# Decoder layer: memory rows and the first key weights loaded and used in halves, one key block more ahead of the stream's rows

## The chip, the cores and the metric

The kernel runs on one core of a Trainium2 chip. The metric is the device time of one execution in microseconds (us). The core has a matrix engine (PE; PEld is its weight load), a vector engine (DVE), a scalar engine (ACT), GpSimd (POOL), and a queue engine (SP) that issues nearly all DMAs here. Every engine works through its own list of instructions in order, and semaphores hold an instruction until what it needs is there.

## The reference, cut to what matters

One decoder layer, batch 1, 1024 tokens, model width 1024, 256 memory tokens. The change touches only the normalisation of the memory and of the stream's rows, and the keys and values of the memory:

```
def rms_norm(x, g):
    y = x * rsqrt(mean(x * x, axis=-1) + 1e-6)
    return y * g

h     = rms_norm(x, norm_mix_pre)            # 1024 x 1024, then h @ w_in
mem_n = rms_norm(mem, norm_mem)              # 256 x 1024
kv    = mem_n @ w_mem_kv                     # 1024 -> 512 keys | 512 values
k_m, v_m = split(kv, 2)                      # 4 heads of 128
s = einsum('bshd,bmhd->bhsm', q, k_m) * 128 ** -0.5
o = einsum('bhsm,bmhd->bshd', softmax(s), v_m)
```

The rest of the layer (differential attention, pooling, gates, output projection, convolutional channel mixer) follows and is the same in both kernels.

## The kernel before

**Names.** Everything is float32, with 128 rows to a tile. Memory rows are two tiles, m0 and m1 (128 x 1024 each, 512 KB), the stream's rows eight tiles, x0 to x7. The key and value weights come as eight blocks of 512 KB: w0 to w3 are 128 key columns each (`rawm0` to `rawm3`), w4 to w7 are 256 rows each of the value weights. `gp` (named g in the load order) is the gain of the stream's norm, `gm` the gain of the memory's norm, turned into a column by the matrix engine (`pg`).

**Load order.** All loads of the first stage are issued by SP in the order of a list of names, `ORDER` (line 33):

```
ORDER = "m0 m1 w0 w1 x0 g x1 w2 x2 w3 x3 x4 w4 x5 x6 w5 x7 w6 w7 q0 u0".split()
```

**First stage (lines 375 to 640), before.** PE first turns the identity matrix ten times into an unused bank (`keep(10)`, tile `idle`), then the gain (`pg`). It transposes all of m0 and m1 in 16 instructions (line 429; tiles `pt` and `pt2`), and three more unused ones. DVE and ACT multiply the transposed pieces by the gain into `memt` (line 442 on DVE, two calls per half and row tile; line 439 on ACT, four pieces). ACT squares the raw memory rows and sums them (line 418), takes the root (line 133), and five small DVE instructions make the reciprocal norms. These are not multiplied into `memt`: DVE spreads them into `rcol` (line 463), PE transposes `rcol` into a row (`pr`, line 469), ACT copies it (`rrow`, line 470), and the keys are scaled with that row afterwards (`keys_scaled`, line 541).

`keys(j)` multiplies weight block j with `memt` over eight slices of 128 into one bank `pk` (line 536). The trace counts each of these float32 products as two PE instructions, so a block has 16. The banks come from a pool of two, so block j+2 may start only when block j's bank has been read by `keys_scaled(j)`. Beside it every row tile of the stream is squared on ACT, its norm found (`norms`), scaled on DVE into `xn` (line 505), transposed on PE (`turn_row`, line 511, 8 instructions) and split into a high and a low part (lines 520 and 524). `values(a, b)` is 16 products of 512 columns into two banks `pv` (line 556), 32 PE instructions.

The order on each engine is the order of the calls at lines 573 to 640: a helper `on(engine, fn)` chains each instruction behind the one called before it on the same engine. So the list of calls is the plan; later stages (`query`, `pool_in` and so on) are ordered by the compiler around it.

Of the kernel before, what the change touches and what calls it, by code (L numbers as in the profile page):

```python
# [15 lines left out]
P = 128  # L16
D = 1024
# [12 lines left out]
C_K = 1024  # L30
PAD = 24
KEEP = (10, 0, 3)
ORDER = "m0 m1 w0 w1 x0 g x1 w2 x2 w3 x3 x4 w4 x5 x6 w5 x7 w6 w7 q0 u0".split()
C_V = 2048
C_U = 3072
C_QM = 3584
# [5 lines left out]
def kernel(  # L42
# [40 lines left out]
    def bank2(shape=(P, 2 * H), name="b2"):  # L83
        return ps2.tile(list(shape), F32, tag="b2", name=name)
# [255 lines left out]
    def chunk(w, c0, n=P):  # L340
        return w[:, c0:c0 + n].rearrange("(k p) c -> p k c", p=P)
# [6 lines left out]
    with tc.tile_pool(name="kvm", reuse_waits="tile", bufs=1, side="right") as kvp:  # L348
# [5 lines left out]
        with tc.tile_pool(name="pa", reuse_waits="tile", bufs=2, side="right") as pa, \  # L354
# [27 lines left out]
            for what in ORDER:  # L382
                if what == "g":
                    gp = pa.tile([P, D], F32, name="gp", bufs=1)
                    nc.sync.dma_start(out=gp, in_=norm_mix_pre[0:1, :].partition_broadcast(P))
                elif what in ("q0", "u0"):
                    ahead[what[0]] = wload(chunk(w_in, C_QM if what == "q0" else C_U), [P, KT, P])
                elif what[0] == "w":
# [23 lines left out]
            def on(engine, fn):  # L412

                with tc.issue_after(order[engine].ins):
                    order[engine] = fn()

            def square(src, acc):
                on("act", lambda: nc.scalar.activation(
                    out=bank2(name="junk"), in_=src, func=AF.Square, accum_out=acc))

            turned = {}
            for i in range(2):
                both = bank2((P, KT, P), "pt2") if i else None
                for g4 in range(2):
                    pt = both[:, 4 * g4:4 * g4 + 4] if i else bank((P, 4, P), "pt")
                    for j in range(4):
                        k = 4 * g4 + j
                        with tc.issue_after(roots["pe"].ins):
                            roots["pe"] = nc.tensor.transpose(pt[:, j, :], xts["m%d" % i][:, k * P:(k + 1) * P], ident)
# [15 lines left out]
            st = small.tile([P, 5, 2], F32, tag="sb2", name="sb", bufs=2)  # L445
            for i in range(2):
                square(xts["m%d" % i], st[:, 0, i:i + 1])
            gained(0, 0, False)
            gained(1, 0, False)
            gained(0, 1, True)  # L450
            gained(1, 1, False)
            with tc.issue_after(order["act"].ins), tc.issue_after(order["dve"].ins):
                rm = rstd_rest(st)

            for e, n in (("dve", "rstd"), ("act", "last")):
                order[e] = roots[n]
            order["pe"] = roots["pe"]
# [4 lines left out]
            for i in range(2):  # L462
                on("dve", lambda: nc.vector.tensor_scalar(
                    out=rcol[:, i, :], in0=ident, scalar1=0.0, scalar2=rm[i], op0=ALU.mult, op1=ALU.add))

            def norms_row():
                pr = bank((P, NM), "pr")
# [97 lines left out]
            def weights_split(name):  # L565
# [22 lines left out]
            keys_scaled(1)  # L588
            highs("x0")
            lows("x0")  # L590
            keys_high(1)
            keys_low(1)
            squares(["x3"], 1, 2)
            norms(["x2", "x3"])
            scaled("x2")
            keys(2)
            turn_row("x1")
            keys_scaled(2)
            highs("x1")
            lows("x1")  # L600
            keys_high(2)
            keys_low(2)
            scaled("x3")
            squares(["x4", "x5"])
            keys(3)
            turn_row("x2")
            keys_scaled(3)
            norms(["x4", "x5"])
            highs("x2")
            lows("x2")  # L610
            keys_high(3)
            keys_low(3)
            scaled("x4")
            squares(["x6"], 0, 2)
            values(0, 4)
            turn_row("x3")
            scaled("x5")
            highs("x3")
            lows("x3")
            squares(["x7"], 1, 2)  # L620
            norms(["x6", "x7"])
            scaled("x6")
            values(4, 7)
            turn_row("x4")
            highs("x4")
            lows("x4")
            scaled("x7")
            values(7, 10)
            turn_row("x5")
            highs("x5")  # L630
            lows("x5")
            weights_split("q")
            values(10, 13)
            turn_row("x6")
            highs("x6")
            lows("x6")
            values(13, 16)
            values_split(0)
            turn_row("x7")
            highs("x7")  # L640
            lows("x7")
# [1139 lines left out]
```

## Time and profile before

| what | value |
|---|---|
| median of 3 runs | 1730.08 us (1729.88 to 1730.09) |
| the profiled execution | 1730.37 us |
| its span on the core | 1728.4 us |
| PE busy | 1713.0 us, 99% |
| DVE, ACT, POOL busy | 72%, 51%, 3% |
| PE from its first transpose of the memory to the first stream row turned | 4.25 to 15.35 us of the span |

The span is the time from the core's first to its last instruction; 1.97 us of the profiled execution lie around it. The profile's views used here are the page, the chain of waits (from the last instruction back to what released it), the timeline of one engine, the DMA issues of a stretch with the time from issue to landing, and busy time by stretches.

### The profile page before, as it was taken

Reading aid. Unit: us, or ns where it says so; the run is one execution under the profiler, and the core shown is the slowest. Engines: PE = TensorE matmul, PEld = TensorE weight load, DVE = VectorE, ACT = ScalarE, POOL = GpSimd, SP = SyncE. Lnnn points to the kernel's source line nnn. Section 1 sums busy time; section 2 is a strip of 40 time slices with the busy share of each in tenths; the row PEclk is TensorE's granted clock in tenths of the full one; section 3 lists DMA queues with packets and bytes.
Section 4 is the critical chain, followed back from the end, with each engine's and each line's share of the span. In section 5 each row is a group of like instructions: output and inputs, shape, how many; then the busy total and the mean of one; then the engine's idle time right before and its main releaser. Section 6 shows DMA issues by size and latency. Waiting matters only on the chain.

```text
span 1728.4 us, 22402 instructions
## 1 busy us (share of the span) xinstructions
PE 1713.0 (99%) x8106; PEld 1420.5 (82%) x8106; DVE 1240.8 (72%) x2047; ACT 886.2 (51%) x1577; POOL 45.0 (3%) x103
## 2 busy tenths in 40 slices
PE   9999999999999999999999999999999999999998
PEld 7888888887888888888888878888888888888886
DVE  6765875666666578888866555848888888878466
ACT  6434554344544467777744344645555555543453
POOL 0000000000000011111110000000000000000000
PEclk9999999999999999999999999999999999999999
DMA  8883544444874686665556571562433322583344
GB/s 280 309 292 114 162 146 143 162 146 152 263 223 155 207 229 176 174 181 150 143 200 228 183 219 49 170 225 92 127 111 104 122 90 94 194 302 102 108 148 141
DMA packets 232803, 294.41 MB, mean 170 GB/s; under 512 B 15865, under 2 KB 161526, under 8 KB 230006
## 3 DMA queue, kind: packets, MB, share of 16 engines
q1 hardware_dynamic: 229158, 285.61, 51.8%
q0 software_dynamic: 3520, 7.38, 1.2%
q8 instruction: 64, 1.05, 0.2%
q14 instruction: 45, 0.37, 0.1%
q10 hardware_dynamic: 16, 0.00, 0.0%
HBM read 201.10 MB, written 85.56 MB: 166 GB/s over the span
## 4 chain that ended last, share of the span: by engine, by line
PE 91%; DVE 5%; DMA 2%; ACT 1%; issue 1%; SPq 0%; DVEq 0%; ACTq 0%
PE pa L98 8%; PE pa L99 8%; PE pa L100 8%; PE pb L99 5%; PE pb L98 5%; PE pb L100 5%; PE pss L1145 3%; PE pd L98 2%; PE pd L99 2%; PE pd L100 2%; PE poa L1201 2%; PE pe L99 2%; PE pe L98 2%; PE pe L100 2%; PE pya L100 2%; PE pya L98 2%
## 5 line engine op out<-in xcount | busy, mean ns | idle before, releaser
L89 ACT ACTIVATE wpage<-s 128x512 fp32r<-128x512 f32 x136 | 85.3, 627 | 107.5 <-DVE s L183 44.6
L90 DVE TENSOR_TENSOR wpage<-s,wpage 128x512 fp32r<-128x512 f32 x136 | 92.7, 687 | 43.3 <-ACT wpage L89 43.3
L1549 DVE SCALAR_TENSOR_TENSOR cvt<-gv,cols,cvt 128x1023 f32<-128x1023 f32 x88 | 112.4, 1278 | 15.7 <-ACT cvt L1545 15.7
L1149 DVE CUSTOM_DVE_ANT_0 z<-pss,hbias 128x256 f32<-128x256 f32 (+7 forms) x128 | 94.5, 752 | 25.1 <-PE pss L1145 23.9
L1154 ACT ACTIVATE z<-z,mx 128x256 f32<-128x256 f32 (+7 forms) x128 | 98.8, 773 | 21.2 <-DVE mx L1149 21.0
L98 PE MATMUL pa<-T,wpage 128*128 128x512 f32 x264 | 102.8, 390 | 0.0
L99 PE MATMUL pa<-T,wpage 128*128 128x512 f32 x264 | 102.7, 389 | 0.0
L100 PE MATMUL pa<-T,wpage 128*128 128x512 f32 x264 | 102.7, 389 | 0.0
L1145 PE MATMUL pss<-ks,q 128*128 128x512 f32 (+5 forms) x384 | 86.6, 349 | 1.4 <-DVE mx L1149 1.4
L89 ACT ACTIVATE page<-blk 128x1024 fp32r<-128x1024 f32 (+1 forms) x42 | 41.5, 990 | 85.2 <-PE pe L99 50.6
L90 DVE TENSOR_TENSOR page<-blk,page 128x1024 fp32r<-128x1024 f32 (+1 forms) x42 | 47.5, 1131 | 38.2 <-ACT page L89 38.1
L1145 PEld LDWEIGHTS pss<-ks,q 128*128 128x128 f32 x384 | 62.9, 189 | 11.1 <-DVE mx L1149 6.2
L98 PE MATMUL pd<-page 128*128 128x512 f32 x176 | 68.6, 390 | 0.5 <-ACT row L1662 0.5
L99 PE MATMUL pd<-page 128*128 128x512 f32 x176 | 68.5, 389 | 0.0
L100 PE MATMUL pd<-page 128*128 128x512 f32 x176 | 68.3, 389 | 0.0
L98 PE MATMUL pa<-hT,wpage 128*128 128x512 f32 x168 | 65.5, 390 | 0.8 <-DVE gq L210 0.8
L100 PE MATMUL pa<-hT,wpage 128*128 128x512 f32 x168 | 65.4, 389 | 0.0
L99 PE MATMUL pa<-hT,wpage 128*128 128x512 f32 x168 | 65.4, 389 | 0.0
L1201 PEld LDWEIGHTS poa<-aT,v 128*128 128x128 f32 x480 | 60.7, 190 | 3.2 <-ACT srow L1221 1.4
L1201 PE MATMUL poa<-aT,v 128*128 128x256 f32 (+1 forms) x480 | 62.6, 281 | 0.0
L98 PEld LDWEIGHTS pa<-T,wpage 128*128 128x128 f32 x264 | 49.5, 188 | 10.6 <-DVE gv L243 0.3
L100 PEld LDWEIGHTS pa<-T,wpage 128*128 128x128 f32 x264 | 49.6, 188 | 10.3
(429 smaller groups left out, 4964.1 us busy)
## 6 DMA issues: line engine op xcount, KB each, us to landing
q<-q_d SPq DMA_DIRECT2D x64, 256.0 KB, 5.2
wd<-in_w_down_dram SPq DMA_DIRECT2D x22, 512.0 KB, 4.6
tw_d<-wd SPq DMA_DIRECT2D x11, 1024.0 KB
rawv<-in_w_up_dram SPq DMA_DIRECT2D x22, 512.0 KB, 5.7
rawu<-in_w_up_dram SPq DMA_DIRECT2D x22, 512.0 KB, 3.9
ff_d<-cvt SPq DMA_DIRECT2D x22, 512.0 KB, 5.1
blk<-ff_d SPq DMA_DIRECT2D x20, 512.0 KB, 7.4
br<-tw_d SPq DMA_DIRECT2D x20, 512.0 KB, 4.9
```

The source lines that it names most:

```text
L89: copy = nc.scalar.activation(out=hi, in_=src, func=AF.Copy)
L90: nc.vector.tensor_tensor(out=lo, in0=src, in1=hi.bitcast(F32), op=ALU.subtract)
L98: nc.tensor.matmul(o, ah, bh, start=first, stop=False, skip_group_check=onto)
L99: nc.tensor.matmul(o, ah, bl, start=False, stop=False, skip_group_check=onto)
L100: return nc.tensor.matmul(o, al, bh, start=False, stop=last, skip_group_check=onto)
L1145: last["scores"] = nc.tensor.matmul(pss[:, i * H:i * H + m], q[:, j, c, ts], keys, start=(j == 0), stop=(j == 1))
L1149: nc.vector.tensor_tensor_reduce(out=halves(z[:, 0:n]), in0=pss.rearrange("p (a m) -> p a m", a=2)[:, 0:parts, 0:m], in1=halves(biases[h][ ...
L1154: nc.scalar.activation(out=z[:, 0:n], in_=z[:, 0:n], func=AF.Exp, scale=-1.0, bias=mx[:, c:c + 1], accum_out=sm if c else sums[:, h, t:t + 1])
L1201: nc.tensor.matmul(po[:, qs], (vh, vl)[i][:, k, :], w[j][:, ws], start=(n == 0), stop=(n == len(terms) - 1))
L1549: nc.vector.scalar_tensor_tensor(out=cv[:, sh:], in0=u[:, 0:S - sh], scalar=w, in1=cv[:, sh:], op0=ALU.mult, op1=ALU.add)
```

## The change

Both memory row tiles and w0 are loaded in two transfers each (256 KB: half of the columns of a row tile, four of the eight slices of w0; the transfers of m0 and m1 then bring 2 KB for a row at a time and not 4 KB). The load order becomes m0a, m1a, w0a, m0b, m1b, w0b, w1, x0, w2, g, x1, w3, x2, x3, x4, w4 and on. PE turns the first halves of m0 and m1, does the first four slices of `keys(0)`, turns the second halves, does the first four slices of `keys(1)`, then the norms' row `pr`, then the second halves of `keys(0)` and `keys(1)`. Before, it turned both rows whole, did six slices of `keys(0)`, `pr`, the other two slices, and `keys(1)`. The three unused transposes behind the memory rows go. After that the keys run one block ahead of the rows: `keys(2)` stands before the turn of x0, `keys(3)` before that of x1, and the values begin before that of x2. The squares of m0 and m1 wait for the second halves, and the squares of x0 stand behind the copy `rrow` on ACT.

```
-ORDER = "m0 m1 w0 w1 x0 g x1 w2 x2 w3 x3 x4 w4 x5 x6 w5 x7 w6 w7 q0 u0".split()
+ORDER = "m0a m1a w0a m0b m1b w0b w1 x0 w2 g x1 w3 x2 x3 x4 w4 x5 x6 w5 x7 w6 w7 q0 u0".split()
...
+                elif what[2:]:
+                    e = "ab".index(what[2])
+                    if what[0] == "w":
...
+                        nc.sync.dma_start(
+                            out=raws[0].rearrange("p (k c) -> p k c", c=P)[:, e * H4:(e + 1) * H4, :],
+                            in_=chunk(w_mem_kv, 0)[:, e * H4:(e + 1) * H4, :])
+                    else:
...
+                        nc.sync.dma_start(out=xts[n][:, hs], in_=mem[int(n[1]) * P:(int(n[1]) + 1) * P, hs])
...
-            for i in range(2):
-                both = bank2((P, KT, P), "pt2") if i else None
-                for g4 in range(2):
+            def turn_memory(g4):
+                for i in range(2):
...
-                keep(KEEP[1 + i])
...
+            keys(0, 0, H4)
+            turn_memory(1)
+            memory_norms()
+            keys(1, 0, H4)
+            norms_row()
             squares(["x0"])
+            keys(0, H4)
+            keys(1, H4)
             norms(["x0"])
-            keys(0, 0, 6)
-            norms_row()
-            keys(0, 6)
             keys_scaled(0)
             scaled("x0")
-            squares(["x1"])
             keys_high(0)
             keys_low(0)
+            keys_scaled(1)
+            squares(["x1"])
+            keys_high(1)
+            keys_low(1)
             norms(["x1"])
             scaled("x1")
-            keys(1)
+            keys(2)
             turn_row("x0")
```

`memory_norms` holds the squares, the second `memt` pieces, the root, the reciprocals and `rcol`, unchanged in themselves.

On PE, at the start of the program, this stood before (`pt` and `pt2` are the turned memory rows, `pk` the keys, `pr` the norms' row, `rawm0` and `rawm1` the weight blocks w0 and w1):

```order
L404 MATMUL pg_185<-ident_80,grow_128 128x8
L429 MATMUL pt_189<-ident_80,xt_132 128x128 x4
L429 MATMUL pt_194<-ident_80,xt_132 128x128 x4
L429 MATMUL pt2_199<-ident_80,xt_134 128x128 x8
L399 MATMUL idle_174<-ident_80 128x128 x3
L536 MATMUL pk_241<-memt_127,rawm0_136 128x256 x6
L469 MATMUL pr_248<-ident_80,rcol_229 128x128 x2
L536 MATMUL pk_241<-memt_127,rawm0_136 128x256 x2
L536 MATMUL pk_269<-memt_127,rawm1_138 128x256 x8
L511 MATMUL pt_278<-ident_80,xn_256 128x128 x4
```

The same place on PE in the changed kernel, up to the first turn of a stream row:

```order
L418 MATMUL pg_188<-ident_80,grow_128 128x8
L444 MATMUL pt_193<-ident_80,xt_132 128x128 x4
L444 MATMUL pt2_192<-ident_80,xt_134 128x128 x4
L553 MATMUL pk_207<-memt_127,rawm0_136 128x256 x4
L444 MATMUL pt_212<-ident_80,xt_132 128x128 x4
L444 MATMUL pt2_192<-ident_80,xt_134 128x128 x4
L553 MATMUL pk_239<-memt_127,rawm1_141 128x256 x4
L486 MATMUL pr_244<-ident_80,rcol_204 128x128 x2
L553 MATMUL pk_207<-memt_127,rawm0_136 128x256 x4
L553 MATMUL pk_239<-memt_127,rawm1_141 128x256 x4
L553 MATMUL pk_282<-memt_127,rawm2_145 128x256 x8
L528 MATMUL pt_291<-ident_80,xn_265 128x128 x4
```

The first products stand behind 8 transposes and not 16, the norms' row `pr` stands behind 8 products and all 16 transposes, and block 2 (`rawm2`) has moved ahead of the first stream row.

On ACT, from the squares of the memory rows to those of x0 and x1, this stood before (`junk` is the squares' thrown-away output, `xt_140` is x0, `xt_144` x1):

```order
L418 ACTIVATE junk_214,sb_211<-xt_134 128x1024
L439 ACTIVATE memt_127<-pt_194,gm_187 128x128 x4
L133 ACTIVATE sb_211<-sb_211,epsilon_85 128x2
L418 ACTIVATE junk_234,stp_233<-xt_140 128x1024
L487 ACTIVATE stp_233<-stp_233,epsilon_85 128x1
L470 ACTIVATE rrow_230<-pr_248 128x256
L418 ACTIVATE junk_258,stp_233<-xt_144 128x1024
```

And this stands there in the changed kernel (`xt_143` is x0, `xt_149` x1):

```order
L432 ACTIVATE junk_224,sb_221<-xt_134 128x1024
L454 ACTIVATE memt_127<-pt_212,gm_190 128x128 x4
L133 ACTIVATE sb_221<-sb_221,epsilon_85 128x2
L487 ACTIVATE rrow_205<-pr_244 128x256
L432 ACTIVATE junk_248,stp_206<-xt_143 128x1024
L504 ACTIVATE stp_206<-stp_206,epsilon_85 128x1
L561 ACTIVATE kmh_117<-kt_263 128x256
L432 ACTIVATE junk_271,stp_206<-xt_149 128x1024
```

The copy `rrow`, which needs PE's `pr`, has moved ahead of the squares of x0. Beyond the first stage the lists of the engines are the same but for some places up to about the 150th row of each, where neighbouring instructions change places.

## Rows read from the trace of the kernel before

**Rows 1.** The page: busy us, share of span, instructions.
```profile
PE 1713.0 (99%) x8106; PEld 1420.5 (82%) x8106; DVE 1240.8 (72%) x2047; ACT 886.2 (51%) x1577; POOL 45.0 (3%) x103
```

**Rows 2.** Chain of waits, first 60 us: start us, us, what.
```profile
0.74 3.46 DMA xt<-in_mem_dram
...
4.25 2.93 PE pt L429 x16
...
7.95 2.86 PE pk L536 x12
10.81 0.22 PE pr L469 x2
11.03 4.32 PE pk L536 x20
15.35 0.87 PE pt L511 x8
...
25.06 3.44 PE pv L556 x8
...
43.17 0.23 PE pq L98
```

**Rows 3.** Timeline of PE: start us, us, instruction, count [idle before, releaser].
```profile
1.41 2.40 PE L399 MATMUL idle<-ident 128*128 128x128 f32 x10 [1.41 <-POOL ident masks.py:199]
3.74 0.27 PE L404 MATMUL pg<-ident,grow 8*128 8x8 f32 x1
...
4.25 2.27 PE L429 MATMUL pt<-ident,xt 128*128 128x128 f32 x10 [0.24 <-DMA xt<-in_mem_dram]
...
6.01 1.16 PE L429 MATMUL pt<-ident,xt 128*128 128x128 f32 x8
```

**Rows 4.** Timeline of DVE and ACT, 4 to 13 us.
```profile
5.40 0.69 DVE L442 TENSOR_TENSOR memt<-pt,gm 128x512 f32<-128x512 f32 x1 [1.19 <-PE pt L429]
...
5.62 1.03 ACT L418 ACTIVATE junk<-xt 128x1024 f32<-128x1024 f32 x1 [0.25 <-DMA xt<-in_mem_dram]
...
6.68 1.12 ACT L439 ACTIVATE memt<-pt,gm 128x128 f32<-128x128 f32 x4
...
7.21 1.29 DVE L442 TENSOR_TENSOR memt<-pt,gm 128x512 f32<-128x512 f32 x2 [1.11 <-PE pt L429]
7.68 0.30 ACT L133 ACTIVATE sb<-sb,epsilon 128x2 f32<-128x2 f32 x1
...
8.48 0.15 DVE L113 RECIPROCAL sb<-sb 128x2 f32<-128x2 f32 x1
...
9.33 0.48 DVE L463 TENSOR_SCALAR rcol<-ident,sb 128x128 f32<-128x128 f32 x2
...
10.49 1.03 ACT L418 ACTIVATE junk<-xt 128x1024 f32<-128x1024 f32 x1 [2.51 <-DMA xt<-in_x_dram]
...
11.67 0.29 ACT L487 ACTIVATE stp<-stp,epsilon 128x1 f32<-128x1 f32 x1
11.87 0.36 ACT L470 ACTIVATE rrow<-pr 128x256 f32<-128x256 f32 x1
12.00 0.16 DVE L491 RECIPROCAL stp<-stp 128x1 f32<-128x1 f32 x1 [0.17 <-ACT stp L487]
...
12.53 0.42 DVE L541 TENSOR_TENSOR kt<-pk,rrow 128x256 f32<-128x256 f32 x1
```

**Rows 5.** Timeline of SP's queue: the issue of w1, and that of w4.
```profile
2.13 0.58 SPq L366 DMA_DIRECT2D rawm<-in_w_mem_kv_dram  x1
...
13.76 0.43 SPq L369 DMA_DIRECT2D rawm<-in_w_mem_kv_dram  x1
```

**Rows 6.** DMA issues, those of w1 and w4: count, size, us to landing.
```profile
rawm<-in_w_mem_kv_dram SPq DMA_DIRECT2D x1, 512.0 KB, 7.1
...
rawm<-in_w_mem_kv_dram SPq DMA_DIRECT2D x1, 512.0 KB, 9.4
```

**Rows 7.** Busy by stretches: us, PE, PEld, DVE, ACT, POOL, PEclk, DMA, GB/s.
```profile
43.00:60.00 17.00, 17.00 (x81) 13.93 (x80) 13.69 (x27) 7.03 (x13) 0.01 (x1) 1.00 0.88 327
```

More of the change, by code (lines that the diff above doesn't have):

```diff
@@ L387 @@
                     ahead[what[0]] = wload(chunk(w_in, C_QM if what == "q0" else C_U), [P, KT, P])
+                elif what[2:]:
+                    e = "ab".index(what[2])
+                    if what[0] == "w":
+                        if e == 0:
+                            raws.append(rawp.tile([P, D], F32, name="rawm0"))
+                        nc.sync.dma_start(
+                            out=raws[0].rearrange("p (k c) -> p k c", c=P)[:, e * H4:(e + 1) * H4, :],
+                            in_=chunk(w_mem_kv, 0)[:, e * H4:(e + 1) * H4, :])
+                    else:
+                        n, hs = what[:2], slice(e * H, (e + 1) * H)
+                        if e == 0:
+                            xts[n] = pa.tile([P, D], F32, tag="xt", name="xt", bufs=8)
+                        nc.sync.dma_start(out=xts[n][:, hs], in_=mem[int(n[1]) * P:(int(n[1]) + 1) * P, hs])
                 elif what[0] == "w":
@@ L421 @@
             turned = {}
-            for i in range(2):
-                both = bank2((P, KT, P), "pt2") if i else None
-                for g4 in range(2):
+            both = bank2((P, KT, P), "pt2")
+            order["pe"] = roots["pe"]
+            def turn_memory(g4):
+                for i in range(2):
                     pt = both[:, 4 * g4:4 * g4 + 4] if i else bank((P, 4, P), "pt")
@@ L427 @@
                         k = 4 * g4 + j
-                        with tc.issue_after(roots["pe"].ins):
-                            roots["pe"] = nc.tensor.transpose(pt[:, j, :], xts["m%d" % i][:, k * P:(k + 1) * P], ident)
+                        on("pe", lambda: nc.tensor.transpose(
+                            pt[:, j, :], xts["m%d" % i][:, k * P:(k + 1) * P], ident))
                     turned[i, g4] = pt
-                keep(KEEP[1 + i])
             def gained(i, g4, act):
@@ L443, in gained, with memory_norms @@
                         out=memt[:, ks, ts], in0=pt, in1=gm[:, ks].unsqueeze(2).to_broadcast([P, 4, P]), op=ALU.mult))
-            st = small.tile([P, 5, 2], F32, tag="sb2", name="sb", bufs=2)
-            for i in range(2):
-                square(xts["m%d" % i], st[:, 0, i:i + 1])
+            turn_memory(0)
             gained(0, 0, False)
             gained(1, 0, False)
[L450 to L457, printed above, removed]
+            rm = []
             rcol = pa.tile([P, 2, P], F32, name="rcol", bufs=1)
             rrow = pa.tile([P, NM], F32, name="rrow", bufs=1)
-            for i in range(2):
-                on("dve", lambda: nc.vector.tensor_scalar(
-                    out=rcol[:, i, :], in0=ident, scalar1=0.0, scalar2=rm[i], op0=ALU.mult, op1=ALU.add))
+            def memory_norms():
+                st = small.tile([P, 5, 2], F32, tag="sb2", name="sb", bufs=2)
+                for i in range(2):
+                    square(xts["m%d" % i], st[:, 0, i:i + 1])
+                gained(0, 1, True)
+                gained(1, 1, False)
+                with tc.issue_after(order["act"].ins), tc.issue_after(order["dve"].ins):
+                    rm.extend(rstd_rest(st))
+                for e, n in (("dve", "rstd"), ("act", "last")):
+                    order[e] = roots[n]
+                for i in range(2):
+                    on("dve", lambda: nc.vector.tensor_scalar(
+                        out=rcol[:, i, :], in0=ident, scalar1=0.0, scalar2=rm[i], op0=ALU.mult, op1=ALU.add))
             def norms_row():
@@ L595 @@
             scaled("x2")
-            keys(2)
+            keys(3)
             turn_row("x1")
-            keys_scaled(2)
+            keys_scaled(3)
             highs("x1")
             lows("x1")
[L601 to L610, printed above, removed]
             keys_high(3)
             keys_low(3)
+            scaled("x3")
+            squares(["x4"], 0, 2)
+            values(0, 4)
+            turn_row("x2")
+            squares(["x5"], 1, 2)
+            highs("x2")
+            norms(["x4", "x5"])
+            lows("x2")
             scaled("x4")
             squares(["x6"], 0, 2)
-            values(0, 4)
+            values(4, 7)
             turn_row("x3")
-            scaled("x5")
             highs("x3")
             lows("x3")
+            scaled("x5")
             squares(["x7"], 1, 2)
@@ L622 @@
             scaled("x6")
-            values(4, 7)
+            values(7, 10)
             turn_row("x4")
@@ L627 @@
             scaled("x7")
-            values(7, 10)
+            values(10, 12)
             turn_row("x5")
@@ L632 @@
             weights_split("q")
-            values(10, 13)
+            values(12, 14)
             turn_row("x6")
             highs("x6")
+            values_split(0)
             lows("x6")
-            values(13, 16)
-            values_split(0)
+            values(14, 16)
             turn_row("x7")
```

6 lines of the change are left out of this document (3 added, 3 removed).

## Prediction

> **What bounds the kernel now.** I read the page first: PE is busy for 1713.0 of 1728.4 us [rows 1], so only some 15 us of the span are not PE's, and a change elsewhere pays only where it lets PE start earlier or takes a gap out. Then the chain of waits over the first 60 us [rows 2]: a DMA of memory rows until 4.20 (0.74 + 3.46), 16 transposes, a DVE pass, and from 7.95 on nothing but PE: keys to 15.35, then rows, keys and values with no gap until the queries begin at 43.17. The stretch after that has PE busy for all of its 17 us [rows 7]. So what counts is when PE finishes the same work: whatever the first stage wins or loses against 15.35 is carried to the end. Third, the timelines of PE, DVE and ACT up to 13 us [rows 3, 4], for how long each step on the way takes, and last when the weights land [rows 5, 6].
>
> The start also runs slowly on PE. Ten transposes of the memory take 2.27 us, 0.227 each, like the ten unused ones before them (0.24); the last eight take 1.16 in all, and a stream row's eight 0.87, 0.109 each [rows 2, 3]. That is a factor of two, the clock's levels of 1.2 and 2.4 GHz, and the change comes near 6.2 us (ten transposes from 4.25 end at 6.52, the last eight begin at 6.01), after PE had worked since 1.41 with a gap of only 0.24 in front of the memory rows.
>
> **The change, step by step.** I write out PE's new list with these durations.
>
> *Start of the keys.* PE is through with `pg` at 4.01 (3.74 + 0.27) [rows 3]. m0a and m1a together are the bytes of m0, which landed at 4.20, so m0a should be there by 4.0 and m1a by 4.2 to 4.3. Eight transposes at 0.227 end at 5.83. DVE's pass began 1.15 after the first of four transposes (5.40 less 4.25), that is 0.24 after they were through; so the second pass, on m1a, begins at 6.07. Before, the first product came 0.74 after the pass that it waited for had begun (7.95 less 7.21) [rows 2, 4]: the keys begin at 6.81, which is 1.14 earlier than 7.95. In between PE idles for about 1.0, where before it did the three unused transposes; these cost nothing, since they stood in the same wait.
>
> *Up to the norms' row.* A product instruction takes 0.216 (4.32 over 20) [rows 2]. Four slices of block 0 are 8 of them: 1.73, to 8.54. The second halves' eight transposes take 0.87, to 9.41 (m0b and m1b are at the place in the load order where m1 ended with w0a added: m1 landed at 5.62, and a block takes 5.62 less 4.20 = 1.4, so m1b lands by about 6.4 and hides). Four slices of block 1: to 11.14. Their w1 keeps its place in bytes; it landed at 9.2 (2.13 + 7.1) [rows 5, 6], 0.2 before its use, so a late w1 moves only work that the next wait absorbs.
>
> *The wait that comes in.* `pr` needs `rcol`, and that hangs on the second halves. m0b's four transposes end at 8.98, ACT begins its four pieces 0.24 later, at 9.22. The root follows 1.00 after them (7.68 less 6.68), the reciprocal 0.33 after the root (12.00 less 11.67), and `rcol` is done 1.33 after that (9.33 + 0.48 less 8.48) [rows 4]: 9.22 + 2.66 = 11.88. The two squares do not hold this up: from 5.62 at about 1.2 each they end near 8.0. PE is free at 11.14 and waits 0.75 for `rcol`. Behind the waiting `pr` stand the second halves of both key blocks, which need neither `rcol` nor anything late; so this wait is paid in full. Before, `rcol` was done at 9.81 and `pr` ran at 10.81 between products, with no wait.
>
> *The sum.* 11.88 + 0.22 for `pr` + 16 products at 0.216 (3.46) = 15.56, and 0.04 for the hand-over: 15.60 against 15.35, a loss of 0.25. So 1.14 is won at the start; the eight transposes that now come after the keys' start take back 0.87, partly repaid by the slow beginning of the old keys (12 products in 2.86, 0.27 more than at 0.216); the wait takes 0.75 and a little more.
>
> *What is late next.* `rrow` now stands before the squares of x0 on ACT. From the end of `pr` at 12.14: about 0.2 to ACT, 0.36 for the copy, 1.18 from a square to its root (11.67 less 10.49), 0.86 to `keys_scaled` (12.53 less 11.67) and 0.42 for it [rows 4]: 15.2. `keys(2)` needs that bank at 15.60. It fits by 0.4; each 0.1 beyond that would cost 0.1. The x0 row itself landed at 10.49 and is turned only at 19.1.
>
> *Values and weights.* `values` begin after 15.60 + two blocks (6.92) + two rows (1.74) = 24.26, where before it was 25.06 [rows 2]. w4 is the 13th block in either load order and landed at 23.2 (13.76 + 9.4) [rows 5, 6]. It hides by 1.1. The rows x1 and x2 come one block later (1.4 us) and are turned 3 us or more after their norms are ready; this is hidden too. From there on the work of PE is the same.
>
> The profiled execution was 1730.37 (span 1728.4 and 1.97 around it); with 0.25 it is 1730.62. The median lies 0.29 below that execution, so I forecast 1730.3. What a measurement of this kernel can tell from no change is about 0.2%, 3.5 us, and the whole stage in question moves by less.
>
> **Rivals.**
>
> *It works without a wait.* If ACT and DVE reach `rcol` before 11.14 (0.75 sooner than I have it), `pr` runs at once: 11.14 + 0.22 + 3.46 = 14.82, a gain of 0.53, 1729.6. For it: my lags are taken from a slower-clocked start. Against it: 2.66 us of chain against 2.16 us of PE work behind m0b's transposes (0.43 for m1b's, 1.73 for the products), and the chain's terms are all measured.
>
> *The halves do not land earlier.* If a quarter lands as late as its whole did (m1a at 5.62), m1's four transposes run from 5.62 to about 6.4 and the keys begin at 7.4; everything shifts by 0.6: a loss of 0.85, 1730.9. For it: a landing needs more than its bytes (3.46 us for a block that takes 1.4). Against it: m1 came only 1.4 after m0, so that fixed part is shared.
>
> *The clock rises late (the other side).* PE's new gap, 5.83 to 6.81, lies where the level changed before. If the lower level holds until `pr`, the first products take 3.46 (to 10.27), m0b's transposes end at 11.18, `rcol` comes at 11.42 + 2.66 = 14.08, PE gets to `pr` at 10.27 + 1.82 + 3.46 = 15.55, and with `pr` at 0.44 and the rest at the higher level it ends at 19.45: a loss of 4.1, 1734.2, slower by 0.24%. It decides from there on; if the level rises on the way, each microsecond at the lower one costs up to half a microsecond. For it: the gap is four times the old one. Against it: the old 0.24 gap did no harm, and PE is busy for 4.4 of the 5.4 us from 1.41 to 6.81. The Trainium skill, "TensorE: Matmul & The Clock Gate", Part 1, says that the throttled state is the default and that activity releases it; the trace agrees in that the transposes halve from 0.227 to 0.109. By that rule a gap at this place can only delay the release.
>
> *The three extra transfers delay everything behind them.* A transfer of 1.4 us of data took 3.46 to land. If that difference of 2.06 were paid anew three times, w4 would land 6.2 later, at 29.4, and PE would wait 5.1 at the values: 1735.4. It decides from a delay of 1.1 on. Against it: m0 and m1 overlapped, as above. The Trainium skill, "DMA: Bandwidth & Descriptors", Rules for kernel authors, asks for at least 1 MiB a transfer for full bandwidth. Its rule speaks against halves of 256 KB; but the trace shows that these transfers overlap in the queue, so I give it little.
>
> **How the numbers follow.** My forecast 0.52, between 1729.9 and 1731.0. No wait 0.20. Halves no earlier 0.08. The clock late in part, up to 2 us lost, 0.11; in full 0.03. Transfers 0.02. What is left, 0.04, is for the reordered neighbours after 43 us, either way. A range from 1729.3 to 1731.9 takes in the forecast, the gain of 0.53 with some room, the late halves and most of the partly late clock. More than 3.5 us slower (over 1733.5) has the full clock case and the transfers, with a part of the rest: 0.05 with rounding. More than 3.5 us faster would need PE to do the first 15 us in less than 12, with some 10 us of work in them: 0.02. Within 0.2% has 0.93.
>
> **What would show it right or wrong.** Right: the first product near 6.8, a wait of PE of 0.5 to 1.0 in front of `pr` released by `rcol`, and the first stream row turned after `keys(2)` near 19.1, which is keys(0) and keys(1) done near 15.6. No wait before `pr`, and that end at 14.8, is the first rival. Transposes of m0b and m1b at 0.22 each, not 0.11, are the late clock; a wait of the first value product on w4 is the transfers. I am wrong altogether if the time moves by more than 3 us, since then something outside this stage has moved.

## The result: 2.9 us slower

| | before | after |
|---|---|---|
| median of 19 runs each | 1730.5 us (1729.6 to 1734.83) | 1733.84 us (1732.27 to 1735.97) |
| the profiled execution | 1730.37 us | 1734.56 us |
| its span | 1728.4 us | 1732.7 us |

The ratio is 1.0017, with a 95% interval of 1.0011 to 1.0024: slower by 2.9 us (1.9 to 4.2); the two medians lie 3.3 apart. The forecast was 1730.3, a loss of 0.25, and its range ended at 1731.9, so the time lies outside it. The profiled execution of after is on the slow side of its own runs; it is 4.2 above that of before, and the medians differ by less.

### The profile after

The page's busy line answers to [rows 1]. PE is busy 1.7 us more in a span that is 4.3 us longer, so more than half of the loss is PE standing still:

```profile
PE 1714.7 (99%) x8103; PEld 1420.9 (82%) x8103; DVE 1240.4 (72%) x2047; ACT 886.8 (51%) x1577; POOL 45.2 (3%) x103
```

The timeline of PE up to the first stream row answers to [rows 2, 3] (start us, us, instruction, count, and in brackets the idle time before and its releaser):

```profile
4.11 2.02 PE L444 MATMUL pt<-ident,xt 128*128 128x128 f32 x8
6.91 3.65 PE L553 MATMUL pk<-memt,rawm 128*128 128x256 f32 x8 [0.78 <-DVE memt L457]
10.40 1.04 PE L444 MATMUL pt<-ident,xt 128*128 128x128 f32 x8
11.27 1.89 PE L553 MATMUL pk<-memt,rawm 128*128 128x256 f32 x8
13.69 0.43 PE L486 MATMUL pr<-ident,rcol 128*128 128x128 f32 x2 [0.52 <-DVE rcol L480]
13.96 7.08 PE L553 MATMUL pk<-memt,rawm 128*128 128x256 f32 x32
20.88 1.04 PE L528 MATMUL pt<-ident,xn 128*128 128x128 f32 x8
```

The keys begin at 6.91, as forecast (6.81), and PE waits for `rcol` in front of `pr`. But the first eight products take 3.65 us, some 0.43 each, where 0.216 was expected: by this pace PE was still at the lower of its two levels until about 10.3 us. The last 16 of the 32 instructions from 13.96 on are `keys(2)`, at 3.46, so keys 0 and 1 are done at 20.88 less 3.46, that is 17.42.

DVE and ACT in the same stretch, which answer to [rows 4]:

```profile
5.26 0.69 DVE L457 TENSOR_TENSOR memt<-pt,gm 128x512 f32<-128x512 f32 x1 [1.05 <-PE pt L444]
...
7.13 1.03 ACT L432 ACTIVATE junk<-xt 128x1024 f32<-128x1024 f32 x1 [4.28 <-DMA xt<-in_mem_dram]
...
11.04 1.14 ACT L454 ACTIVATE memt<-pt,gm 128x128 f32<-128x128 f32 x4 [1.58 <-PE pt L444]
...
13.26 0.48 DVE L480 TENSOR_SCALAR rcol<-ident,sb 128x128 f32<-128x128 f32 x2
```

DVE has one instruction for each half row tile that it multiplies by the gain (m0a, m1a and m1b; ACT has m0b). ACT's first square can start only when m0b is there, at 7.13; whole, m1 had been there at 5.62 [rows 4]. SP's queue, which answers to [rows 5], shows what stands ahead of w1:

```profile
0.74 0.86 SPq L401 DMA_DIRECT2D xt<-in_mem_dram  x2
1.66 0.43 SPq L394 DMA_DIRECT2D rawm<-in_w_mem_kv_dram  x1
2.13 0.97 SPq L401 DMA_DIRECT2D xt<-in_mem_dram  x2
3.15 0.43 SPq L394 DMA_DIRECT2D rawm<-in_w_mem_kv_dram  x1
3.62 0.51 SPq L366 DMA_DIRECT2D rawm<-in_w_mem_kv_dram  x1
```

Three more issues at 0.43 to 0.5 each, and w1 is issued at 3.62, not 2.13. The transfers themselves are slower too. Busy time by stretches of before (columns as in [rows 7]; the last is GB/s):

```profile
2.00:4.00 2.00, 2.00 (x10) 1.58 (x8) 0.00 (x0) 0.84 (x2) 0.00 (x0) 1.00 0.95 328
4.00:6.00 2.00, 1.76 (x9) 1.75 (x9) 0.76 (x2) 1.52 (x3) 0.00 (x0) 1.00 1.05 356
```

The same stretches of after, and the next one:

```profile
2.00:4.00 2.00, 2.00 (x10) 1.59 (x8) 0.00 (x0) 0.84 (x2) 0.00 (x0) 1.00 0.82 235
4.00:6.00 2.00, 1.91 (x9) 1.43 (x8) 0.86 (x2) 0.00 (x0) 0.00 (x0) 1.00 0.93 304
6.00:8.00 2.00, 1.22 (x4) 0.92 (x4) 0.69 (x1) 0.87 (x1) 0.00 (x0) 1.00 0.89 268
```

235 GB/s against 328, with the DMA engines busy for 0.82 of the stretch and not 0.95. (The granted clock stands at 1.00 even where the products take twice their time. I read the level from the pace of like instructions there; that the slow pace is the clock's lower level is a reading that the column does not confirm.)

Behind the first stage a second loss appears. The change also gave out the 16 values differently: 4, 3, 3, 2, 2, 2 over six gaps between the rows, and before 4, 3, 3, 3, 3 over five. Rows x5 and x6 and the first query on PE; before, the rows from x4 on came every 3.45 us without a wait (`hTl` is the low part of a turned row, `vml` that of the values):

```profile
37.40 1.88 PE L573 MATMUL pv<-rawm,memt 128*128 128x512 f32 x4
39.69 1.25 PE L528 MATMUL pt<-ident,xn 128*128 128x128 f32 x8 [0.41 <-DVE hTl L541]
40.78 1.88 PE L573 MATMUL pv<-rawm,memt 128*128 128x512 f32 x4
42.50 1.04 PE L528 MATMUL pt<-ident,xn 128*128 128x128 f32 x8
43.37 1.88 PE L573 MATMUL pv<-rawm,memt 128*128 128x512 f32 x4
45.64 0.50 PE L98 MATMUL pq<-hTh,wh 128*128 128x512 f32 x1 [0.38 <-DVE vml L578]
```

DVE in that stretch, where one row costs it an `xn` and two `hTl`, some 2.4 us:

```profile
31.45 0.17 DVE L508 RECIPROCAL stp<-stp 128x2 f32<-128x2 f32 x1 [1.95 <-ACT stp L504]
...
32.12 1.28 DVE L541 TENSOR_TENSOR hTl<-pt,hTh 128x512 fp32r<-128x512 f32 x2
33.32 1.27 DVE L522 SCALAR_TENSOR_TENSOR xn<-xt,stp,gp 128x1024 f32<-128x1024 f32 x1
34.51 1.28 DVE L541 TENSOR_TENSOR hTl<-pt,hTh 128x512 fp32r<-128x512 f32 x2
```

So only two products (four instructions, 1.72 us) stand between the turns of x4, x5, x6 and the queries. A turn with them takes PE 2.6 us, barely more than a row takes DVE, and DVE had just lost 1.95 us to a root that ACT, since the change, has behind x2's copies. PE waits for DVE, twice before 60 us and once more at 75 us (`ptl` is the low part of the memory attention's turned weights):

```profile
75.43 0.39 PE L98 MATMUL pss<-kmh,qh 128*128 128x256 f32 x1 [0.64 <-DVE ptl L90]
```

### A ledger

I cut the timelines of PE into three pieces: A, to the first stream row's turn (less 3.46 where `keys(2)` stands ahead of it); B, from there to the first product of `pu`; C, from that to the first of `py`, tiles of two later stages. (The timeline's start of the first row lies 0.16 before the chain's 15.35.)

| profiled execution | A | B | C |
|---|---|---|---|
| before | 15.19 | 40.04 | 117.83 |
| after | 17.42 | 41.44 | 118.68 |
| e1_fill, e2_norms, e3_both, e8_w1 (after's start, mended in parts) | 16.20, 16.15, 16.08, 15.65 | 41.45, 41.19, 41.20, 41.48 | 118.34, 117.92, 118.73, 118.65 |
| e4_gap, e14_w0 (before's start and order) | 15.92, 14.98 | 40.20, 40.39 | 117.61, 117.70 |
| e5_halves, e7_loads, e13_rows (half rows, before's order later) | 17.30, 18.23, 17.81 | 39.96, 39.86, 39.91 | 117.69, 117.65, 117.63 |
| e6_ahead (whole loads, after's order later) | 16.61 | 41.45 | 118.88 |
| e9_spread (e6 with two edits) | 16.30 | 40.58 | 118.68 |
| e10_all, e15_whole | 15.85, 18.81 | 40.92, 40.59 | 117.79, 117.77 |

After less before: 2.23 + 1.40 + 0.85 = 4.48 of the span's 4.3. B holds to its kind of order within half a microsecond; A moves by one or two from execution to execution of like starts, so on A only timed ratios decide. So it is with what lies behind C: it is 1553.3 to 1557.7 over all profiles, 1557.7 and 1554.4 in e11_rows and e13_rows, which are one kernel.

### The profile page after: what moved, and what is told of

The parts are those of the page before. It is cut to its first block, busy times and chain, and to the rows that moved or that the text cites. A ratio compares the mean times of both kernels' runs of the same rounds, so it can differ in the third digit from the quotient of the medians.

```text
span 1732.7 us, 22401 instructions
## 1 busy us (share of the span) xinstructions
PE 1714.7 (99%) x8103; PEld 1420.9 (82%) x8103; DVE 1240.4 (72%) x2047; ACT 886.8 (51%) x1577; POOL 45.2 (3%) x103
## 4 chain that ended last, share of the span: by engine, by line
PE 86%; DVE 6%; DMA 4%; ACT 2%; issue 1%; SPq 1%; DVEq 0%; ACTq 0%
PE pa L98 8%; PE pa L100 8%; PE pa L99 8%; PE pb L98 5%; PE pb L100 5%; PE pb L99 5%; PE pss L1167 3%; PE pd L98 2%; PE pd L100 2%; PE pd L99 2%; PE poa L1223 2%; PE pe L100 2%; PE pe L98 2%; PE pe L99 2%; PE pout L99 1%; PE pout L100 1%
## 5 line engine op out<-in xcount | busy, mean ns | idle before, releaser
L1167 PEld LDWEIGHTS pss<-ks,q 128*128 128x128 f32 x384 | 62.9, 189 | 11.1 <-DVE mx L1171 6.2
L99 PEld LDWEIGHTS pa<-T,wpage 128*128 128x128 f32 x264 | 49.6, 188 | 10.3
```

The source lines that it names most:

```text
L99: nc.tensor.matmul(o, ah, bl, start=False, stop=False, skip_group_check=onto)
L1167: last["scores"] = nc.tensor.matmul(pss[:, i * H:i * H + m], q[:, j, c, ts], keys, start=(j == 0), stop=(j == 1))
```

## Experiments

All but two (e11_rows and e12_w0, a single run each) were timed over several rounds beside the kernel before. Three causes stood against each other: PE's late level, late transfers, and the new order behind the first stage.

**The gap that PE stands idle in, filled.** After, with four unused transposes behind the first halves:

```
             turn_memory(0)
+            for j in range(4):
+                on("pe", lambda: nc.tensor.transpose(idle[:, j % 4, :], ident, ident))
```

> The changed kernel with four unused transposes put behind the first halves' turns, where PE idles from about 6.0 to 6.9 us; all else as changed. Theory 1 (the gap delays the rise of PE's clock, so the first eight products run at 0.43 us each and not 0.216): the products behind the gap run at 0.216, the second halves' turns begin near 8.7 and not 10.4, the first stream row is turned near 19.1 and not 20.9, and the time falls by about 1.8 us against the changed kernel. Rival (what is late is the landing of the second halves and weights, not the clock): the turns of the second halves still begin near 10, and the time moves by less than 0.5 us.

Measured: 1733.51, ratio 1.0018 (1.0009 to 1.0027). The timeline of PE:

```profile
6.91 1.99 PE L555 MATMUL pk<-memt,rawm 128*128 128x256 f32 x8 [0.33 <-DVE memt L457]
8.74 1.04 PE L444 MATMUL pt<-ident,xt 128*128 128x128 f32 x8
10.73 1.96 PE L555 MATMUL pk<-memt,rawm 128*128 128x256 f32 x8 [0.95 <-DMA rawm<-in_w_mem_kv_dram]
```

The products run at the higher level, 1.99 for 3.65, and PE then waits 0.95 for w1. In the profile the filler brought 1.2 us (first row 19.66 for 20.88), in the median nothing that can be told: after's ratio and this one together resolve about 1.9 us. So the late level is not the cause of the whole 2.9, which is there without it. A smaller part, or one in some executions only, is not excluded.

**The root ahead of the copies.** After, with the norms of x4 and x5 in front of x2's copies on ACT:

```
             squares(["x5"], 1, 2)
-            highs("x2")
             norms(["x4", "x5"])
+            highs("x2")
```

> The changed kernel with the norms of x4 and x5 called ahead of highs of x2, as before the change; only ACT's order moves (the root ahead of the two copies of x2's high part). Theory 2 (ACT's root stands behind copies that wait for PE's turn of x2, so DVE idles about 2 us near 29.5 to 31.4 us and then runs late until the queries): that idle time goes, PE's waits for hTl and vml near 39 and 45 us (0.4 each, some 1.2 us in all with the small ones) go, and the time falls by about 1.2 us. Rival (DVE is late there only because the whole stage started 2 us late, with the rows bunched): the waits stay, less than 0.4 us gained.

Measured: 1733.9, ratio 1.0017 (1.0009 to 1.0026), where 1.2 us less than after was expected. DVE's idle 1.95 is gone, and B falls by 0.25 only. The start, not edited here, is of interest:

```profile
3.94 1.67 PE L444 MATMUL pt<-ident,xt 128*128 128x128 f32 x8
6.66 1.97 PE L553 MATMUL pk<-memt,rawm 128*128 128x256 f32 x8 [1.05 <-DMA rawm<-in_w_mem_kv_dram]
...
10.68 1.97 PE L553 MATMUL pk<-memt,rawm 128*128 128x256 f32 x8 [1.17 <-DMA rawm<-in_w_mem_kv_dram]
```

After's own start with its whole gap, yet at the higher level from the first product. But here the level had risen before the gap: the eight transposes take 1.67, not 2.02, the last of them at the faster pace. So this says nothing of a gap at the lower level. And both halves of the keys wait for weights, 2.2 us together.

**Both edits**, e1's and e2's:

> The changed kernel with both edits: the four unused transposes in the gap, and the root of x4 and x5 ahead of x2's copies. If theories 1 and 2 are both right and independent, the gains add: about 3 us faster than the changed kernel, level with the kernel before within 0.5 us. If a third cause beyond 46 us of the span matters, 0.5 to 1 us of the loss stays.

Measured: 1732.93, ratio 1.0012 (1.0004 to 1.0021). PE waits 0.65 for w1 at 10.61. That is 0.9 below after's median in another session, within what the intervals leave open, and not the 3 that were expected.

**The unused transposes by themselves.** The kernel before, without the three behind the memory rows (`KEEP = (10, 0, 3)` becomes `(10, 0, 0)`):

> The kernel before without its three unused transposes behind the memory rows, so that PE idles there from about 7.0 to 7.95 us. The clock has risen near 6.2 us there. If a gap of 0.9 us does harm only where the clock has not yet risen (theory 1), the time stays within 0.3 us. If any gap of that size lowers the clock, the products behind it run at 0.43 us and the time rises by 1.5 us or more.

Measured: 1729.63, ratio 0.9998 (0.999 to 1.0007). They cost and bring nothing that can be measured. In this execution, against what was expected, the level had not risen when the gap came:

```profile
4.23 3.68 PE L429 MATMUL pt<-ident,xt 128*128 128x128 f32 x16 [0.22 <-DMA xt<-in_mem_dram]
8.69 2.86 PE L536 MATMUL pk<-memt,rawm 128*128 128x256 f32 x12 [0.78 <-DVE memt L442]
```

All 16 transposes run at the slow pace, PE is idle for 0.78, and the products behind it run at the fast one. After has an idle time of 0.78 behind slow transposes too, and slow products behind it. So a gap of this size by itself does not decide the level, though after's comes 1.8 us earlier.

**The halves and the new start alone.** After, with the loads behind w1 and the calls behind the first `keys_scaled` in before's order:

```
-ORDER = "m0a m1a w0a m0b m1b w0b w1 x0 w2 g x1 w3 x2 x3 x4 w4 ...
+ORDER = "m0a m1a w0a m0b m1b w0b w1 x0 g x1 w2 x2 w3 x3 x4 w4 ...
...
-            keys(2)
             turn_row("x0")
...
-            keys(3)
+            keys(2)
             turn_row("x1")
```

> One part alone: memory rows and w0 in halves and the new start on PE up to the second halves of blocks 0 and 1; from there on load order and calls as before the change (no key block ahead, the values spread 4, 3, 3, 3, 3). Theory A (the start loses about 0.9 us, since w1 is issued 1.5 us later behind three more issues and lands near 10.7 us, where PE waits for it; the other 1.3 us are lost among the late rows by the new order): PE waits for w1, the first stream row is turned near 16.2 and not 15.35 (later by 1 to 1.5 if the clock rises late in the profiled execution), no wait for hTl or vml near 39 to 45 us, and the time is 0.8 to 1.5 us above the kernel before. Rival B (the whole loss is the start's): 2.5 us or more above before.

Measured: 1732.28, ratio 1.0012 (1.0003 to 1.0021), 2.1 us. The timeline of PE:

```profile
5.45 0.66 PE L444 MATMUL pt<-ident,xt 128*128 128x128 f32 x4 [0.43 <-DMA xt<-in_mem_dram]
7.19 1.97 PE L553 MATMUL pk<-memt,rawm 128*128 128x256 f32 x8 [1.08 <-DMA rawm<-in_w_mem_kv_dram]
...
11.10 1.97 PE L553 MATMUL pk<-memt,rawm 128*128 128x256 f32 x8 [1.07 <-DMA rawm<-in_w_mem_kv_dram]
...
17.30 1.09 PE L528 MATMUL pt<-ident,xn 128*128 128x128 f32 x8 [0.55 <-DVE xn L522]
```

At the higher level from 5.45 on, and still A is 2.1 behind before's, by four waits, three of them for transfers. m1a, forecast for 4.2 to 4.3, holds its transposes until 5.45. The order later on is undisturbed (B 39.96).

**The block ahead alone.** The kernel before with whole loads and its own start, w2 loaded ahead of g, and after's calls behind the second part of `keys(0)`:

```
-            keys(1)
+            keys(2)
             turn_row("x0")
...
-            keys(2)
+            keys(3)
             turn_row("x1")
```

> The other part alone: the start of the kernel before with whole loads, but w2 ahead of the gain in the load order, block 1 and block 2 ahead of the first row, and all calls behind as in the changed kernel (one key block ahead, the values spread 4, 3, 3, 2, 2, 2). Theory A: the first row is turned where 15.35 + 3.46 = 18.8 says, then PE waits for hTl at x5 and for vml before the queries, 1.2 to 1.6 us in all, and the time is 1.2 to 1.8 us above the kernel before. Rival B: no such waits, since the rows are not late here, and the time is within 0.4 us of before.

Measured: 1732.07, ratio 1.0014 (1.0005 to 1.0022), 2.4 us. The waits of PE up to 100 us (in all, times, longest):

```profile
PE pk L536 <- DVE rcol L463: 2.5, 1, 2.5
PE idle L399 <- POOL ident masks.py:199: 1.4, 1, 1.4
PE ptx L724 <- DVE ptl L90: 0.8, 1, 0.8
PE pt L511 <- DVE hTl L524: 0.4, 1, 0.4
PE pq L98 <- DVE vml L561: 0.4, 1, 0.4
```

The last three are after's late waits, without any half transfer. (The first stands at the first product, at 9.42. It is put down to `rcol`, which no product reads; what they lack then is most likely w0, issued as before: w1, next in the queue, lands at 10.99 for 9.19, and in e9_spread the same wait ends with w0's transfer.) So the second part of the change has a loss of its own.

**The loads alone.** The kernel before, its order of work untouched, with only m0, m1 and w0 in halves, in after's order (`m0a m1a w0a m0b m1b w0b w1 x0 g x1 w2 ...`):

> The kernel before with only its loads of m0, m1 and w0 cut in halves, in the order m0a, m1a, w0a, m0b, m1b, w0b; PE, ACT and DVE as before. If the halves move more slowly as such, the bytes moved in the first 8 us fall below the 304 to 356 GB/s of before as in the changed kernel (235 to 304), w1 lands near 10.7 us, and the first transposes of whole rows wait for m0b until about 7 us: the keys begin near 9.5 to 10, 2 us later than 7.95, and the time rises by about 2 us. If the halves move as fast as wholes, m0b and m1b are there by 6 us and the loss is below 1.2 us.

Measured: 1731.93, ratio 1.0013 (1.0004 to 1.0022). PE waits 2.50 for m0b in the profile, and the granted clock falls after it (columns as in [rows 7]):

```profile
8.00:10.00 2.00, 2.00 (x13) 1.85 (x10) 0.35 (x1) 1.97 (x6) 0.00 (x0) 0.56 1.14 365
10.00:12.00 2.00, 1.86 (x7) 1.38 (x6) 1.77 (x8) 1.00 (x5) 0.00 (x0) 0.59 1.02 404
```

**w1 sooner.** After with `m1b w1 w0b` in the load order:

> The changed kernel with w1 loaded ahead of w0b (which is needed only behind the norms' row). Theory A (PE is held by w1's landing): w1 lands about 1 us sooner, the wait for it shrinks to 0.3 or less where the clock rose early, and the norms' row or its rcol takes its place; 0.4 to 0.8 us faster than the changed kernel. Rival (the chain of rcol holds PE anyway): less than 0.3 us.

Measured: 1733.5, ratio 1.002 (1.0011 to 1.0029). In the profile the wait for w1 shrinks to 0.18 and A is 15.65, 0.2 above the forecast's; the median gains nothing. A miss, and one whose profile alone would have misled.

**The values spread.** e6 with the values in pieces of 2, 3, 3, 3, 3, 2 and e2's root:

```
-            values(0, 4)
+            values(0, 2)
             turn_row("x2")
...
-            values(10, 12)
+            values(8, 11)
             turn_row("x5")
```

> The kernel with the key block ahead and the start of before, with the values spread 2, 3, 3, 3, 3, 2 over the gaps between the rows' turns (instead of 4, 3, 3, 2, 2, 2) and the root of x4 and x5 ahead of x2's copies. Theory (with only two products between the turns of x4, x5 and x6 PE needs 2.6 us a row, as much as DVE needs, so that every DVE delay ends on PE): with three, 3.45 us a row, the wait of x5's turn for hTl (0.4, and the same again for its second half) goes; what is left is the wait for vml before the queries at most. The time falls by 0.8 to 1.4 us against the same kernel without this spread, to 0.5 to 1.2 us above before. Rival (DVE's total work is the limit, not where PE's products stand): the waits only move to another row, less than 0.3 us gained.

Measured: 1730.81, ratio 1.0001 (0.9992 to 1.001). The wait before x5's turn is gone; the 0.4 at the queries stays. B falls from 41.45 to 40.58, and the median is that of before. So the loss of e6 comes from how the work is given out between the rows, and giving it out evenly takes it back, by the medians; the two intervals just overlap. The edit is two in one, but the root alone took only 0.25 off B in e2_norms.

**Everything mended, half rows kept.** After with e1's filler, e8's order of w1, and e9's edits:

> The changed kernel with all four repairs: unused transposes in the gap, w1 ahead of w0b, the root ahead of x2's copies, the values spread 2, 3, 3, 3, 3, 2. If the causes found (late landing of halves and of w1, late clock in some executions, too few products between late rows) are the whole loss: the first row is turned near 19.1, no wait for hTl at x5, and the time is within 0.7 us of before. If a further cause sits behind 50 us of the span: 1.5 us or more above before.

Measured: 1732.87, ratio 1.0012 (1.0003 to 1.0021). PE's waits up to 60 us are 0.2 to 0.4 each, A is 15.85 and B 40.92 in the profile, and still it is 2 us slower. By e9_spread beside it, what is left is most likely the start's; the intervals of the two overlap.

**Which half costs.** The kernel before with only the memory rows in halves (`m0a m1a m0b m1b w0 w1 ...`), and with only w0 in halves (`m0 m1 w0a w0b w1 ...`). First a single run of each:

> The kernel before with only m0 and m1 loaded in halves, m0a, m1a, m0b, m1b (2 KB for a row), and w0 whole behind them. If the half rows themselves move slowly: 235 to 255 GB/s between 2 and 4 us as in every kernel with halves, and not 328 to 340. If it is w0's short pieces moved forward that slow those: 320 GB/s or more between 2 and 4 us.

> The kernel before with only w0 loaded in halves, behind whole memory rows. If the half rows are what moves slowly: 328 to 340 GB/s between 2 and 4 us and the keys begin near 8 as before. If the number of transfers in the queue is what slows the start: under 300 GB/s between 2 and 6 us and w1 later by more than 0.5 us.

They gave 1735.54 and 1730.12, and 282 and 354 GB/s from 2 to 4 us; single runs are too little to settle it. Timed over rounds, the rows in halves:

> The kernel before with only m0 and m1 loaded in halves (m0a, m1a, m0b, m1b), timed. If the half rows of 2 KB carry the cost of the halves: 1.5 to 2.5 us above before. If the cost is mainly w0's halves or the number of issues: less than 0.7 us.

Measured: 1732.47, ratio 1.0011 (1.0002 to 1.002). PE, then the stretch of 2 to 4 us:

```profile
4.43 1.12 PE L443 MATMUL pt<-ident,xt 128*128 128x128 f32 x4 [0.42 <-DMA xt<-in_mem_dram]
6.92 2.79 PE L443 MATMUL pt<-ident,xt 128*128 128x128 f32 x12 [1.38 <-DMA xt<-in_mem_dram]
```

```profile
2.00:4.00 2.00, 2.00 (x10) 1.58 (x8) 0.00 (x0) 0.84 (x2) 0.00 (x0) 1.00 0.74 243
```

w0 in halves:

> The kernel before with only w0 loaded in halves behind whole memory rows, timed. If the half rows carry the cost: within 0.5 us of before, or a little faster, since the first products then wait for half of w0 only in executions in which w0 lands late. If w0's halves carry it: 1 us or more above before.

Measured: 1729.62, ratio 0.9995 (0.9986 to 1.0003). The same stretch:

```profile
2.00:4.00 2.00, 2.00 (x10) 1.58 (x8) 0.00 (x0) 0.84 (x2) 0.00 (x0) 1.00 0.92 328
```

So of the cut loads it is the rows that cost, under before's order of work. m0b lands at 6.9 where whole rows were both there by 5.62, and the data rate is that of after, with the DMA engines busy for 0.74 of the stretch and not 0.92. w0's halves have the same 256 KB and one more issue, but keep their pieces of 512 B, and cost nothing that can be measured. Whether the shorter pieces do it, or two more transfers where w0 has one, was not separated. And these turns wait for m0b (1.38 here, 2.50 in e7_loads), which after's do not; so what the half rows cost in after is not shown by these two.

**The new start with whole rows.** e10 with `m0 m1 w0a w0b w1 x0 ...`:

> The changed kernel with the repairs of the last study (fill, root ahead, values spread 2, 3, 3, 3, 3, 2), but with m0 and m1 loaded whole and only w0 in halves. PE's order at the start is that of the changed kernel. If the half rows are the cost that is left: within 0.7 us of before, 1.3 us or more below the kernel with the same repairs and half rows. If the new order at the start costs by itself: 1.3 us or more above before.

Measured: 1733.42, ratio 1.0015 (1.0006 to 1.0024), 2.6 us. No cure, against the reading that half rows are the whole of the start's loss; by the terms set beforehand, this is the outcome for a cost of the new order itself. In its profile PE waits 1.60 for w0a, and then comes this:

```profile
8.32 3.33 PE L555 MATMUL pk<-memt,rawm 128*128 128x256 f32 x8 [1.60 <-DMA rawm<-in_w_mem_kv_dram]
```

```profile
8.00:10.00 2.00, 1.68 (x5) 1.43 (x6) 0.00 (x0) 0.00 (x0) 0.00 (x0) 0.69 1.05 349
10.00:12.00 2.00, 2.00 (x7) 1.54 (x7) 0.00 (x0) 0.00 (x0) 0.00 (x0) 0.50 1.16 305
```

One reading, which was not tested: 8 of the 16 transposes that used to stand ahead of the first product, and so beside w0's landing, now come after it. And w0 itself was late: in this profile, e6_ahead and e9_spread, the three with whole rows and w2 ahead of g, w1 landed at 10.6 to 11.0, in the four with whole rows and g ahead at 9.1 to 9.4. w2 and g are issued only at 5.5 or later, and why this should matter, or whether it is chance, is not shown. No version beat the kernel before beyond its interval; e14_w0 has the lowest median, and its interval takes in no change.

## Why the prediction was wrong

**Right.** The start of the keys (6.91 for 6.81), the idle time before it (0.78 for about 1.0), and the chain to `rcol`, 2.70 from ACT's first piece (11.04) to its end for 2.66, with a wait of PE before `pr` (0.52 for 0.75). That the keys began at 6.91 was in part luck: the forecast had no term for w0a, which held them in other executions. Leaving out the unused transposes cost nothing that can be measured (e4_gap). And x1's and x2's rows, which load later, kept no PE instruction waiting.

**Wrong, the first step: the landings.** "m1b lands by about 6.4 and hides" and "w1 keeps its place in bytes" reckoned a transfer's landing from its bytes, and w0a's landing was put at nothing without a reason. Half rows moved at 235 GB/s for 328 in the stretch of 2 to 4 us, and in all ten profiles with half rows at 235 to 282, in the seven with whole rows at 328 to 354. By 8 us the ten had moved 1.6 to 1.7 MB, the seven 2.0 to 2.1 (sums of the stretches). m0b alone came at 7.13; w0a kept PE waiting in e2_norms and e5_halves (to 6.66 and 7.19), and w1, issued 1.49 later, held PE in four profiles until 10.6 to 11.1, where 9.2 was reckoned.

The rival of halves that do not land earlier came true in part: in e5_halves and e8_w1 m1a's transposes waited until 5.45 and 5.32, near the 5.62 of the whole. I had written that a late w1 "moves only work that the next wait absorbs". It absorbs little: e1_fill's `pr` ran at 12.53, with no wait left, 0.65 behind the forecast's 11.88. The rival of the extra transfers had the right kind of harm and looked for it at w4; it reached PE at w0a and w1. The cut loads alone, under before's order of work, cost 2 us in the median (e7_loads, e13_rows). The Trainium skill, "DMA: Bandwidth & Descriptors", Rules for kernel authors, asks for at least 1 MiB a transfer. The runs bear its direction out for the rows; w0's halves, as small, go against it, so size by itself isn't what decided here. I had given that rule little weight.

**Wrong, the second step: "From there on the work of PE is the same."** The same instructions, but not the same filling. I compared when values and weights are due and not how long PE works between two rows, against DVE's 2.4 us a row. e6_ahead prices this at 2.4 us (0.9 to 3.8) and e9_spread takes it back. The prediction had counted a move outside the first stage only as what a change of more than 3 us would mean. In the profiles it is 1.4 in B and, in five of the nine kernels with the block ahead, another wait for `ptl` of 0.2 to 0.8 near 73 to 89 us.

**The rival of the late clock** happened in the very execution that was profiled, and by its size: 1.66 on the eight products, 1.2 at the first row. It had a plausible mechanism, and without e1_fill it would have been the explanation. Its sign, slow transposes of m0b and m1b, did not show: the level rose just before them. With the gap filled and the level higher the median was as slow, so it is not the whole loss; whether it is some part, below the 1.9 us that the rounds resolve, stays open. The same gap stands behind slow transposes in e4_gap and was followed by fast products.

**The sum.** The forecast was 0.25. Alone, the start costs 2.1 (e5_halves, 0.5 to 3.6) and the order later on 2.4 (e6_ahead, 0.9 to 3.8); together 2.9 (1.9 to 4.2). The parts add up within these bounds, and no closer.

**Open.** How the start's 2 us divide between slower half rows, the later issue of w1, the new order and lost clock. e8_w1, which took w1's wait away in its profile, gained nothing in the median; and in e14_w0 w1 was issued 0.55 later than before and landed at 9.1 all the same. e15_whole shows that whole rows alone don't mend it in the new order; its profile names the wait for w0a and the lower clock behind it, but one profile of a start that varies by 1 to 2 us does not show that for the median. Not tried: the new order with the memory's and w0's loads issued from another queue.

## What to carry to other kernels

Cutting a load in order to begin sooner pays only if each piece lands in proportion to its bytes; time the cut loads alone, with the work untouched, before building on them. When work is drawn ahead of a stream, compare what is left between two of its rows with the slowest other engine's time for a row. And a cause read from one profile of a start that varies needs a timed run without it: here taking the most visible one away brought nothing that the rounds could tell.

## What was not expected of the hardware

- With a memory row's 4 KB cut into two pieces of 2 KB the first transfers ran some 14 to 34% slower (235 to 282 for 328 to 354 GB/s, 2 to 4 us), while w0's halves left the rate as it was (328 and 354). In e13_rows, where only the rows were cut, the DMA engines were busy for 0.74 and 0.72 of 2 to 4 and 4 to 6 us; in e14_w0 for 0.92 and 1.03.
- When PE comes to its higher level, by the pace of like instructions, differs from execution to execution: about 6.2 us before, 10.3 after, between 4.6 and 12.3 over all profiles, and in e11_rows and e13_rows, which are one kernel, at 12.3 and 10.7.
- Having reached it, PE can lose it again: behind waits of 2.50 and 1.60 us the granted clock of the next stretches was 0.56 and 0.59 (e7_loads), 0.69 and 0.50 (e15_whole). Yet behind a wait of 2.45 us in e6_ahead it stayed at 1.00, with the products at their fast pace.
